# Two-layer hybrid decoder trunk on one core: low parts of the MLP's middle tiles on VectorE, and other buffers for the second pair of raw quad weights

## The chip, the cores and the metric

The kernel runs on one core of one Trainium2 chip. The metric is the device time of that core in microseconds (us), from a run of the whole program; lower is better. A core has a matrix engine (TensorE, PE in the profile), three engines for elementwise work (VectorE: DVE, ScalarE: ACT, GpSimd: POOL), and SyncE (SP), which here issues loads. Each engine has a queue of its own and works it off in order; between engines the program waits on semaphores. Matrix products accumulate in PSUM; all else lies in SBUF.

## The reference

Two layers (`DEPTH = 2`), a sequence of 512 tokens, model width 1024, everything in float32. Each layer mixes tokens with three parallel groups of heads and then runs an MLP; only the MLP is touched here:

```python
        x = x + mixed @ w_out[l]

        h = rms_norm(x, norm_mlp_g[l])
        x = x + jnp.square(jax.nn.relu(h @ w_mlp_up[l])) @ w_mlp_down[l]
    return rms_norm(x, final_norm_g)
```

`w_mlp_up` is 1024 x 4096, `w_mlp_down` 4096 x 1024.

## The kernel before

**Layout and precision.** Activations lie transposed: a tile is 128 features by 512 tokens, so x is 8 tiles, the middle of the MLP 32 tiles ("mids"). A float32 product is made of three matmuls on a shorter format: each operand is split into a high part (a cast, on ScalarE) and a low part (the operand less its high part, a subtraction of two SBUF tiles), and high x high, high x low and low x high are added up in PSUM. So every weight tile that is loaded costs a load on SyncE's queue, a cast on ScalarE and a subtraction, mostly on VectorE (`weights`, L333; `both`, L1488; `split` inside `quad`, L1577).

**Up projection.** The first four mids are plain products (`up`). The other 28 are made two at a time by `two` (L1478): a 2x2 scheme that needs seven half-size products where the plain one needs eight. It forms sums of weight blocks (s1 to s4; s1 and s3 of the later pairs come ready-made from an accumulating load that GpSimd issues, L1476), seven products into the PSUM tiles pa, pb and pc (12 matmuls of 256 columns each), and copies such as `c1`, which ScalarE takes out of PSUM (L1545) before the next product may accumulate further on pa. Then `square` applies relu, the norm's factor (VectorE, L1417) and the square (ScalarE, L1418), and `kept` (L1403) splits the mid into high part `mh` (ScalarE, L1408) and low part `ml` (L1409): for the first four mids of a layer on VectorE, for the other 28 on GpSimd.

**Down projection.** It runs in halves: `down(h, ...)` multiplies four mids (h counts 0 to 7) into four of the eight x tiles. For the (h, half) listed in `DN_QUADS`, six in layer 0 and four in layer 1, `quad` (L1573) does it with the same seven-product scheme; `turn_blocks` forms the sums of mids that it needs. Elsewhere plain products (dn) of 512 columns are used. A quad works on two pairs of x tiles, i = 0 and i = 1. For each pair it loads two raw weight tiles r0 and r1 (`rawq`, L1610), splits r0 (whi/wlo "a"), forms the sums s2q and s4q on VectorE (L1614 to L1618), splits those (shi/slo "b" and "c") and a part of r1 (whi/wlo "d"). The last reader of a pair's raw tiles is one of the sums or the low part "d". Then the products of both pairs run interleaved; p1q, p5q, u2q and c1q are copies from PSUM on ScalarE (L1599), and all additions to x are on VectorE.

**Buffers.** The four raw tiles of a quad come from the ring "raw" of three buffers of 128 x 512 float32, which the plain weights' raw tiles use too. A ring "sq" of two buffers of the same size holds squares of x for the norms: in the mixer, and at the end of the MLP (last down half of layer 0, last group of layer 1).

**Order.** The mixer's order of work is written out by hand (`ORDER`, with `SLOTS` for its buffers). The MLP's is not: the framework orders each engine's instructions when the program is built, from the order in the source and its own plan, so casts and sums of one product can stand ahead of copies of another, and parts of `two` and `quad` interleave.

Of the kernel before, what the change touches and what calls it, by code (L numbers as in the profile page):

```python
# [10 lines left out]
F32 = mybir.dt.float32  # L11
# [5 lines left out]
ALU = mybir.AluOpType  # L17
# [6 lines left out]
P = 128  # L24
# [249 lines left out]
def tile_trunk(ctx: ExitStack, tc: tile.TileContext, xT, wts, prm_d, cst_d, lora_d, gup_d, lam_d, fin_d, hd_d, out):  # L274
    nc = tc.nc
    act, dve, pool = nc.scalar, nc.vector, nc.gpsimd
# [23 lines left out]
    wp = Pool(ctx.enter_context(tc.tile_pool(name="wp", bufs=2)), "wp")  # L300
# [3 lines left out]
    def psum(tag, bufs, name):  # L304
        return ps.tile([P, 512], F32, tag=tag, bufs=bufs, name=name)
# [23 lines left out]
    WB = 3  # L329
# [238 lines left out]
    for l in range(L):  # L568
# [826 lines left out]
        with ExitStack() as mx:  # L1395
# [7 lines left out]
            def kept(m):  # L1403

                i = len(mids)
                hi = fp.tile([P, S], F32R, tag="mh", bufs=RING, name=f"mh{l}_{i}")
                lo = fp.tile([P, S], F32R, tag="ml", bufs=RING, name=f"ml{l}_{i}")
                act.copy(hi, m)  # L1408
                (dve if i < 4 else pool).tensor_tensor(lo, m, hi.bitcast(F32), ALU.subtract)  # L1409
                mids.append((hi, lo))  # L1410

            def square(cs, name, side=ALU.max):

                m = fp.tile([P, S], F32, tag="m", bufs=4, name=f"m{name}")
                for i, c in enumerate(cs):
                    q = slice(i * H, i * H + c.shape[1])
                    dve.scalar_tensor_tensor(m[:, q], c, 0.0, rs[:, q], side, ALU.mult)  # L1417
                act.activation(m, m, AF.Square)  # L1418
                kept(m)
                return m  # L1420
# [152 lines left out]
            def quad(h, half):  # L1573
# [3 lines left out]
                def split(src, pool_, tags, bufs, name):  # L1577
                    hi, lo = [pool_.tile([P, 4, P], F32R, tag=t, bufs=bufs, name=f"{t}{l}_{h}_{name}")[:, :src.shape[1]] for t in tags]
                    act.copy(hi, src)
                    dve.tensor_tensor(lo, src, hi.bitcast(F32), ALU.subtract)  # L1580
                    return hi, lo
# [23 lines left out]
                for i in range(2):  # L1605
                    j = 4 * half + 2 * i
                    n = f"{l}_{h}_{j}"
                    r0, r1 = [wp.tile([P, 4, P], F32, tag="raw", bufs=WB, name=f"rawq{n}_{c}") for c in range(2)]
                    for c, r in enumerate((r0, r1)):
                        nc.sync.dma_start(r.rearrange("p k c -> p (k c)"),  # L1610
                                          wts[wbase + NG_IN + NG_OUT + NG_UP + 8 * g + j + c, :, k0 * P:(k0 + 4) * P])
                    w0 = split(r0, wp, ("whi", "wlo"), WB, f"{j}a")
                    s = [fp.tile([P, 4, P], F32, tag=t, name=f"{t}q{n}") for t in ("s2", "s4")]
                    dve.tensor_tensor(s[0][:, :2], r1[:, 0::2], r1[:, 1::2], ALU.add)  # L1614
                    dve.tensor_tensor(s[0][:, 2:], s[0][:, :2], r0[:, 0::2], ALU.subtract)
                    s12 = split(s[0], fp, ("shi", "slo"), 5, f"{j}b")
                    dve.tensor_tensor(s[1][:, :2], r0[:, 0::2], r1[:, 0::2], ALU.subtract)
                    dve.tensor_tensor(s[1][:, 2:], r0[:, 1::2], s[0][:, 2:], ALU.subtract)  # L1618
                    s34 = split(s[1], fp, ("shi", "slo"), 5, f"{j}c")
                    w22 = split(r1[:, 1::2], wp, ("whi", "wlo"), WB, f"{j}d")  # L1620
                    pts = [psum(t, b, f"q{c}{n}")[:, :H] for c, t, b in zip("abc", (("rp", "rp", "at"), ("mm", "mm", "at"))[i],
                                                                          ((4, 4, 2), (2, 2, 2))[i])]
                    ab.append((j, w0, s12, s34, w22, pts))
                for step in ((0, 1), (2, 3), (5, 4), (6,)):
                    for j, w0, s12, s34, w22, (pa, pb, pc) in ab:
                        n = f"{l}_{h}_{j}"
# [28 lines left out]
            def down(h, js):  # L1655

                if (h, js[0] // 4) in DN_QUADS[l]:
                    quad(h, js[0] // 4)
                    return
                g, k0 = h // 2, 4 * (h % 2)  # L1660
                if h == 0 and js[0] == 0:
                    pts = [psum(("at", "mm")[j], 2, f"dn{l}_{h}_{j}") for j in js[:2]]
                    ws = [list(weights(wbase + NG_IN + NG_OUT + NG_UP + 8 * g + j, k0, k0 + 4)) for j in js[:2]]
                    for a, b in ((0, 3), (3, 4)):
                        for j, pt, w in zip(js, pts, ws):
                            for k in range(a, b):
                                (whi, wlo), (ahi, alo) = w[k], mids[k]
                                pe.matmul(pt, whi, ahi, start=(k == 0), stop=False)
                                pe.matmul(pt, whi, alo, start=False, stop=False)
                                pe.matmul(pt, wlo, ahi, start=False, stop=(k == 3))  # L1670
                    for j, pt in zip(js, pts):
                        dve.tensor_tensor(x[j], pt, x[j], ALU.add)
                    js = js[2:]
                for j in js:
                    pt = psum(*(("mm", 2), ("rp", 4))[j % 2], f"dn{l}_{h}_{j}")
                    mm3(pt, weights(wbase + NG_IN + NG_OUT + NG_UP + 8 * g + j, k0, k0 + 4), mids[4 * h:4 * h + 4], 4)
                    dve.tensor_tensor(x[j], pt, x[j], ALU.add)
                    if h == 2 * N_KG - 1 and j < NK - LATE:
                        norm_tile(j, f"m{l + 1}")
# [92 lines left out]
```

## Time and profile before

| | us |
|---|---|
| median of 3 runs | 1237.47 (1237.47 to 1239.9) |
| the profiled execution | 1238.0, its span 1236.2 |
| MLP of layer 0 in the span, about | 276 to 600 |
| MLP of layer 1, about | 900 to 1227 |

The rows that carry the argument stand in the prediction. In rows of groups, the number after the bar is the busy time, then the mean of one instruction in ns, then the idle time of its engine just before and what ended it. In rows of the timeline the first number is the start in us from the span's start, the second the duration; brackets hold the engine's idle time before it and what released it. In rows of windows: the length, then busy times of PE, PE's weight loads, DVE, ACT and POOL (with counts), the clock granted to TensorE as a share, the DMA engines' mean busy share and GB/s. In rows of waits: who <- for whom: us in total, times, longest.

### The profile page before, as it was taken

The page shows a single profiled execution, that of the slowest core. Times are in us where ns is not written, and L with a number is a line of the kernel's source. Part 1 is how long each engine was busy: PE and PEld are TensorE (multiplying, and loading weights), DVE is VectorE, ACT ScalarE, POOL GpSimd, SP SyncE. Part 2 cuts the span into 40 slices and gives each one's busy share as a digit, 9 for nine tenths or more (in the row PEclk, how much of TensorE's full clock was granted, in tenths as well). Part 3 has the DMA queues.
Part 4 walks back from the last instruction along what each step waited for, and adds up shares of the span by engine and source line. Part 5 has one row for each costly group of instructions (what it writes and reads, how often), then busy time and mean ns, then how long its engine had stood idle before and what let it go on. Part 6 is the DMA issues. An engine that isn't in the chain of part 4 may idle for free. (4 is left out here: it accounts for less than half of the span.)

```text
span 1236.2 us, 26900 instructions
## 1 busy us (share of the span) xinstructions
PE 1217.8 (99%) x10090; PEld 1065.6 (86%) x10090; DVE 1011.3 (82%) x2023; ACT 742.6 (60%) x1606; POOL 386.0 (31%) x502
## 2 busy tenths in 40 slices
PE   9999999999999999999999999999999999999997
PEld 7788788888999989889888888888889898998987
DVE  7787888879888998989867777787897999899654
ACT  7785755557456655656675656564775566565543
POOL 2264636331122121121126354553302212222111
PEclk9999999999999999999999999999999999999998
DMA  6523333125653463631235243322456645446122
GB/s 225 159 90 108 111 86 102 53 96 169 190 146 108 128 180 98 168 86 52 94 113 159 82 133 118 94 70 69 145 172 147 152 110 158 128 118 177 54 78 77
DMA packets 95506, 148.48 MB, mean 120 GB/s; under 512 B 22544, under 2 KB 26384, under 8 KB 95376
## 3 DMA queue, kind: packets, MB, share of 16 engines
q1 hardware_dynamic: 87168, 132.39, 34.5%
q0 software_dynamic: 7488, 13.63, 7.2%
q8 instruction: 79, 1.29, 0.5%
q10 hardware_dynamic: 720, 0.75, 0.2%
q14 instruction: 51, 0.42, 0.1%
HBM read 137.56 MB, written 9.18 MB: 119 GB/s over the span
## 5 line engine op out<-in xcount | busy, mean ns | idle before, releaser
L694 POOL TENSOR_TENSOR wlo<-raw,whi 128x512 fp32r<-128x512 f32 x84 | 112.1, 1336 | 203.8 <-ACT whi L682 167.3
L287 PE MATMUL pj<-ahim,whi 128*128 128x512 f32 x392 | 156.7, 400 | 0.0
L287 PE MATMUL pj<-ahim,wlo 128*128 128x512 f32 x392 | 156.5, 399 | 0.0
L287 PE MATMUL pj<-alom,whi 128*128 128x512 f32 x392 | 156.0, 398 | 0.0
L1476 POOL DMA_DIRECT2D s<-wts x52 | 48.0, 922 | 293.3 <-DVE slo_p L1491 68.5
L1409 POOL TENSOR_TENSOR ml<-m,mh 128x512 fp32r<-128x512 f32 x56 | 82.3, 1518 | 178.9 <-ACT mh L1408 63.1
L682 ACT CAST whi<-raw 128x512 fp32r<-128x512 f32 x142 | 87.6, 618 | 70.3 <-PE pj L287 26.5
L287 PE MATMUL dn<-mh,whi 128*128 128x512 f32 x288 | 112.3, 390 | 0.0
L287 PE MATMUL dn<-ml,whi 128*128 128x512 f32 x288 | 112.2, 390 | 0.0
L287 PE MATMUL dn<-mh,wlo 128*128 128x512 f32 x288 | 112.1, 390 | 0.0
L1490 ACT CAST shi_p<-s 128x512 fp32r<-128x512 f32 x112 | 70.0, 625 | 65.1 <-PE pa L287 35.1
L287 PE MATMUL pa<-thi,shi_p 128*128 128x256 f32 x336 | 95.6, 285 | 4.5 <-ACT c L1545 3.9
L287 PE MATMUL pa<-tlo,shi_p 128*128 128x256 f32 x336 | 94.8, 282 | 0.0
L287 PE MATMUL pa<-thi,slo_p 128*128 128x256 f32 x336 | 94.4, 281 | 0.0
L1491 DVE TENSOR_TENSOR slo_p<-s,shi_p 128x512 fp32r<-128x512 f32 x112 | 76.5, 694 | 17.8 <-ACT shi_p L1490 16.6
L348 ACT CAST whi<-raw 128x512 fp32r<-128x512 f32 x86 | 52.9, 620 | 56.2 <-PE dn L287 30.7
L287 PEld LDWEIGHTS pj<-alom,whi 128*128 128x128 f32 x392 | 73.9, 188 | 14.0 <-issue 0.5
L287 PEld LDWEIGHTS pj<-ahim,wlo 128*128 128x128 f32 x392 | 73.9, 188 | 13.8 <-issue 0.2
L287 PEld LDWEIGHTS pj<-ahim,whi 128*128 128x128 f32 x392 | 73.8, 188 | 13.7 <-issue 0.3
L349 DVE TENSOR_TENSOR wlo<-raw,whi 128x512 fp32r<-128x512 f32 x86 | 72.5, 846 | 10.7 <-ACT whi L348 10.7
L1490 ACT CAST shi_p<-raw 128x512 fp32r<-128x512 f32 x84 | 52.4, 624 | 33.6 <-PE pb L287 18.1
L287 PEld LDWEIGHTS pa<-thi,shi_p 128*128 128x128 f32 x336 | 63.0, 188 | 6.1 <-ACT c L1545 4.7
(649 smaller groups left out, 3905.2 us busy)
## 6 DMA issues: line engine op xcount, KB each, us to landing
raw<-wts SPq DMA_DIRECT2D x323, 256.0 KB, 2.8
s<-wts SPq DMA_DIRECT2D x52, 256.0 KB, 3.6
s<-wts POOLq DMA_DIRECT2D x52, 256.0 KB, 4.4
rawq<-wts SPq DMA_DIRECT2D x40, 256.0 KB, 2.9
qs<-dqhi SPq DMA_DIRECT2D x24, 128.0 KB, 3.4
ks<-dkhi SPq DMA_DIRECT2D x24, 128.0 KB, 3.6
x<-xT SPq DMA_DIRECT2D x8, 256.0 KB, 4.8
dqhi<-qhi SPq DMA_DIRECT2D x6, 256.0 KB, 3.2
```

Source lines behind the costliest of these rows:

```text
L287: ins = nc.tensor.matmul(*a, **k)
L348: act.copy(hi[:, :n], raw[:, :n])
L349: (pool if a and lean[0] else dve).tensor_tensor(lo[:, :n], raw[:, :n], hi[:, :n].bitcast(F32), ALU.subtract)
L682: yield act.copy(hi[:, k0:k1], raw[:, k0:k1])
L694: yield eng.tensor_tensor(lo[:, k0:k1], raw[:, k0:k1], hi[:, k0:k1].bitcast(F32), ALU.subtract)
L1409: (dve if i < 4 else pool).tensor_tensor(lo, m, hi.bitcast(F32), ALU.subtract)
L1476: pool.dma_start(t.rearrange("p k c -> p (k c)"), of[1], accum_op=ALU.add)
L1490: act.copy(hi, src)
L1491: dve.tensor_tensor(lo, src, hi.bitcast(F32), ALU.subtract)
```

## The change

Two lines. In `kept`, the low part of every mid is made on VectorE, so 28 subtractions a layer change their engine. In `quad`, the raw tiles r0 and r1 of the second pair (i = 1) come from the ring "sq" with its two buffers; those of the first pair stay in "raw" with its three.

```diff
                 act.copy(hi, m)
-                (dve if i < 4 else pool).tensor_tensor(lo, m, hi.bitcast(F32), ALU.subtract)
+                dve.tensor_tensor(lo, m, hi.bitcast(F32), ALU.subtract)
                 mids.append((hi, lo))
...
                 for i in range(2):
                     j = 4 * half + 2 * i
                     n = f"{l}_{h}_{j}"
-                    r0, r1 = [wp.tile([P, 4, P], F32, tag="raw", bufs=WB, name=f"rawq{n}_{c}") for c in range(2)]
+                    r0, r1 = [wp.tile([P, 4, P], F32, tag=("raw", "sq")[i], bufs=(WB, 2)[i], name=f"rawq{n}_{c}") for c in range(2)]
```

No other line changes; the number of matmuls, loads, casts and subtractions is the same.

## The prediction

> **What bounds the kernel now.** I read the head of the page first, then TensorE's own waits, then the windows by stage, then the groups on VectorE and GpSimd, and at the end the order of time around two of the waits.
>
> ```profile
> span 1236.2 us, 26900 instructions
> PE 1217.8 (99%) x10090; PEld 1065.6 (86%) x10090; DVE 1011.3 (82%) x2023; ACT 742.6 (60%) x1606; POOL 386.0 (31%) x502
> ```
>
> TensorE is busy for all but 18.4 us of the span, and the change removes no matmul. So it can only win back stalls of TensorE, or add some. Where those 18.4 us lie (columns: PE, PEld, DVE, ACT, POOL busy):
>
> ```profile
> 276.00:600.00 324.00, 319.75 (x2212) 297.02 (x2211) 290.97 (x535) 195.00 (x396) 66.40 (x57) 1.00 0.48 131
> 900.00:1181.00 281.00, 277.34 (x1931) 258.67 (x1930) 241.92 (x437) 162.71 (x332) 58.94 (x51) 1.00 0.50 133
> 1227.00:1236.20 9.20, 1.70 (x16) 1.32 (x16) 2.84 (x12) 1.52 (x4) 1.62 (x3) 0.67 0.59 194
> ```
>
> The two MLP stretches, the only ones that the diff touches, lose 4.25 and 3.66 us; 7.5 us are the output tail, which stays. VectorE is 90% busy in the first stretch. Who is late is in the list of TensorE's waits:
>
> ```profile
> PE pa L287 <- ACT c L1545: 3.9, 4, 1.2
> PE qa L287 <- ACT p1q L1599: 2.9, 4, 0.9
> ```
>
> So there are eight stalls that matter, 6.8 us together, all behind a PSUM copy on ScalarE. They come as pairs: p1q inside a second quad of an h, c some 15 us later. One place in order of time shows what such a stall costs in full:
>
> ```profile
> 434.04 0.28 PE L287 MATMUL pb<-alof,shi_p 128*128 128x256 f32 x1
> 434.15 0.28 PE L287 MATMUL pb<-ahif,slo_p 128*128 128x256 f32 x1
> 435.34 0.39 PE L287 MATMUL pa<-thi,shi_p 128*128 128x256 f32 x1 [0.91 <-ACT c L1545]
> 435.56 0.28 PE L287 MATMUL pa<-tlo,shi_p 128*128 128x256 f32 x1
> ```
>
> Such matmuls run at a step of about 0.12 (434.04 to 434.15). Here the steps are 1.19 and then 0.22: 1.07 + 0.10 = 1.17 lost, where the list says 0.91. With 0.26 more for each, the eight cost 6.8 + 8 x 0.26 = **8.9 us**: about all that can be won.
>
> **Why ScalarE is late: two causes.** First p1q:
>
> ```profile
> 410.05 0.33 SPq L343 DMA_DIRECT2D raw<-wts  x1
> 410.42 0.43 SPq L1610 DMA_DIRECT2D rawq<-wts  x1
> ```
> ```profile
> 414.88 0.43 DVE L1614 TENSOR_TENSOR s2q<-rawq 128x256 f32<-128x256 f32 x1 [2.05 <-DMA rawq<-wts]
> ```
> ```profile
> 416.06 0.62 ACT L1579 CAST shi_6b<-s2q 128x512 fp32r<-128x512 f32 x1 [3.83 <-DVE s2q L1615]
> 417.40 0.62 ACT L1408 CAST mh<-m 128x512 fp32r<-128x512 f32 x1
> 418.75 0.62 ACT L1408 CAST mh<-m 128x512 fp32r<-128x512 f32 x1
> 419.79 0.37 ACT L1599 COPY p1q<-qa 128x256 f32<-128x256 f32 x1
> ```
>
> The last raw tile of the quad's second pair is asked for at 410.42 only, because three "raw" buffers hold four tiles and this one waits for the sums of the first pair (L1618) to let go. VectorE stands 2.05 us for it, ScalarE 3.83 behind that. ScalarE then works off a row without a gap, and p1q, whose matmuls were over, is copied at 419.79; TensorE waits for it.
>
> Then c:
>
> ```profile
> 433.59 0.69 DVE L1499 TENSOR_TENSOR s<-s,raw 128x512 f32<-128x512 f32 x1
> ```
> ```profile
> 434.39 0.62 ACT L1490 CAST shi_p<-s 128x512 fp32r<-128x512 f32 x1 [2.22 <-PE pb L287]
> 434.92 0.37 ACT L1545 COPY c<-pa 128x256 f32<-128x256 f32 x1
> ```
>
> ```profile
> 414.88:434.28 19.40, 18.72 (x155) 18.26 (x153) 19.40 (x38) 13.41 (x30) 4.09 (x3) 1.00 0.43 124
> ```
>
> The view names PE as the releaser of that cast, but it reads a sum s that VectorE finished at 434.28, so I put it to VectorE. In the window from 414.88 to there VectorE is busy 19.40 of 19.40 us: it is a backlog. The copy of c stands behind that cast in ScalarE's queue.
>
> **Part 1: 56 low parts of mids go from GpSimd to VectorE.** What they cost today and what they disturb:
>
> ```profile
> L1409 POOL TENSOR_TENSOR ml<-m,mh 128x512 fp32r<-128x512 f32 x56 | 82.3, 1518 | 178.9 <-ACT mh L1408 63.1 <-DVE wlo_2d L1580 32.4 <-issue 28.4
> L1409 DVE TENSOR_TENSOR ml<-m,mh 128x512 fp32r<-128x512 f32 x8 | 5.5, 689 | 0.5 <-ACT mh L1408 0.5
> L349 DVE TENSOR_TENSOR wlo<-raw,whi 128x512 fp32r<-128x512 f32 x86 | 72.5, 846 | 10.7 <-ACT whi L348 10.7
> L1499 DVE TENSOR_TENSOR s<-s,raw 128x512 f32<-128x512 f32 x28 | 27.0, 965 | 0.0
> L1499 DVE TENSOR_TENSOR s<-raw,s 128x512 f32<-128x512 f32 x28 | 25.1, 895 | 0.4
> L1566 DVE TENSOR_TENSOR dlo<-ta,dhi 128x512 fp32r<-128x512 f32 x10 | 9.8, 984 | 0.0
> L1561 DVE TENSOR_TENSOR ta<-m,ta 128x256 f32<-128x256 f32 x10 | 9.6, 959 | 0.0
> L1562 DVE TENSOR_TENSOR tb<-m,m 128x256 f32<-128x256 f32 x10 | 9.2, 921 | 0.0
> L1580 DVE TENSOR_TENSOR wlo_6d<-rawq,whi_6d 128x256 fp32r<-128x256 f32 x5 | 7.5, 1509 | 0.0
> ```
> ```profile
> 323.86 3.85 DVE L349 TENSOR_TENSOR wlo<-raw,whi 128x512 fp32r<-128x512 f32 x1
> 396.59 0.42 DVE L1580 TENSOR_TENSOR wlo_2d<-rawq,whi_2d 128x256 fp32r<-128x256 f32 x1
> 410.27 0.68 DVE L1580 TENSOR_TENSOR wlo_6a<-rawq,whi_6a 128x512 fp32r<-128x512 f32 x1
> 410.88 0.42 DVE L1541 TENSOR_TENSOR c<-pc,p 128x256 f32<-128x256 f32 x1
> 416.82 0.42 DVE L1417 SCALAR_TENSOR_TENSOR m<-c,rsf 128x256 f32<-128x256 f32 x1
> 418.76 1.46 DVE L1499 TENSOR_TENSOR s<-s,raw 128x512 f32<-128x512 f32 x1
> 420.14 1.51 DVE L1580 TENSOR_TENSOR wlo_6d<-rawq,whi_6d 128x256 fp32r<-128x256 f32 x1
> ```
> ```profile
> 418.16 3.21 POOL L1409 TENSOR_TENSOR ml<-m,mh 128x512 fp32r<-128x512 f32 x2 [5.32 <-PE qc L287]
> ```
>
> *Added*: back to back, a 128x512 subtraction advances VectorE by 0.60 (410.27 to 410.88; its record of 0.68 overlaps the next). 56 x 0.60 = 33.6 us; by the record's 0.689 it would be 38.6. I take 0.60, since the queue is what counts.
> *Given back*: VectorE's instructions with two SBUF inputs stretch while GpSimd computes. The two at 418.76 and 420.14 lie on GpSimd's pair (418.16 to 421.37) and take 1.46 for 0.69 and 1.51 for 0.43; the one at 323.86 took 3.85. Over the groups, (mean less 0.689, or 0.43 for 256 columns) x count: L349 13.5, L1499 7.7 and 5.8, L1566 3.0, L1561 5.3, L1562 4.9, wlo_6d 5.4: **45.6 us**. All of it can't be charged with certainty to these 56, so the bounds are 0 and 45.6; I take 45.6, since each group is an MLP line and GpSimd has no other arithmetic there. VectorE's net is 33.6 - 45.6 = **12 us less** in the two stretches, by the other end 33.6 more.
>
> The Trainium skill, page "SBUF — State Buffer", section on engine ports, says that VectorE and GpSimd lock a shared port pair for a whole instruction, and that an instruction of VectorE with two SBUF inputs blocks against one of GpSimd that reads SBUF. The 3.85 us at 323.86 agree. By that rule alone each of the 56 could block VectorE for up to 1.518, 85 us; the rows show about half, since many start beside instructions that read PSUM. Against this, the skill's "VectorE: DVE Perf Modes" gives (N+151)/0.96 ns for such an instruction, 691 ns at 512: an estimate of 56 x 0.691 = 38.7 us added and 7 us net saved. The record agrees with that length, but the queue advances by 0.60.
>
> *Moved*: the 56 leave GpSimd's queue, where they stood ahead of the accumulating loads of s; those can only start earlier. A new ml on VectorE waits for its copy mh on ScalarE. Behind it stand c0q, the sums s and slo_p, on which casts and TensorE wait. If ml stands right behind the m that is squared, it waits: VectorE was through m at 417.24 (416.82 + 0.42), the copies end at 418.02 and 419.37, so some 0.8 + 0.75 = 1.5 us a pair, and nothing if it stands later. The matmuls that read ml come a half of the down projection later, so its delay itself costs nothing. I take 0.3 a pair on the path in the quads' stretches, nearer to none, because the eight that VectorE does already idled 0.5 us in all (row above).
>
> **Part 2: raw tiles of the second pair in "sq".** No instruction is added. Those two buffers were last read by wlo_2d of the quad before, at 396.59 (row above), so the load of 410.42 can go up to 13 us earlier. VectorE's waits of this kind:
>
> ```profile
> DVE s2q L1614 <- DMA rawq<-wts: 9.5, 6, 2.4
> ```
>
> I expect 8 to 9.5 of these to go (nothing if SyncE reaches the load no earlier). "sq" is otherwise used in the MLP only for norms at its end, when no quad runs. In layer 0, twelve tiles change ring; twelve is a multiple of 2 and 3, so the later buffers stay the same.
>
> **The sum.** The p1q stalls, 2.9 + 4 x 0.26 = 3.9, go with the late tile. The c stalls, 3.9 + 4 x 0.26 = 4.9, go if VectorE is over 1.1 us earlier at 433.59: 2.05 of gap and (0.77 + 1.08 - 1.2) = 0.65 of contention make 2.7, less 0.3 for new waits. That is 8.9. Against it I set 2 us for new stalls: a rebuilt order on three engines, 28 pairs, a quarter of them with 0.3 us. What is late next is the tail, and TensorE itself. 1238.0 (the profiled execution) - 6.9 = **1231** us; the median of the three runs, 1237.47, is 0.5 lower, within what the estimate can tell.
>
> **The rivals.**
> *Only the tile part works* (the backlog stays because ml waits about as long as the contention it removes): 1238.0 - 3.9 = 1234. For it: VectorE is 90% busy. Against it: 2.7 us of slack where 1.1 is needed.
> *The change doesn't do what it says*: SyncE's queue is in order, and the load of the last raw tile stays behind others that wait (the one before it, 410.05, waits too), or gains and new stalls cancel: 1236 to 1239, say 1238.
> *Slower: head of line on VectorE.* With every pair of ml right behind m, 1.5 us of wait plus 1.2 of work against 1.85 of contention is 0.85 a quad; in ten quads, where VectorE has no gap, 8.5 us; less 3.9 of part 2: 1242.6. It decides from about 0.65 us of wait a pair on. For it: m, square, copy and ml are a chain, and a planned order can put ml early. Against it: VectorE has 9.5 us of waits to fill.
>
> **How the numbers follow.** Forecast, 1228.5 to 1233.5: 0.50. Tile part only, 1233.5 to 1235.5: 0.17. No change, 1235.5 to 1239.5: 0.17. Slower, about 1242.6: 0.16. A measurement of this kernel can tell about 0.2%, 2.5 us. Below 1235.0 lie the forecast and three quarters of the second case: faster 0.63; slower 0.15; same 0.22. The range runs from 1228, all eight stalls gone and the small ones too, to 1241, which leaves out about 0.13 above and little below; the likeliest case's own is 1228.5 to 1233.5.
>
> **What would show it.** Part 1 right: no VectorE record over 1 us in the MLP, mean of L349 near 0.69, GpSimd's busy time 82 lower, VectorE's 0 to 15 lower. Part 2 right: the wait of s2q for rawq gone. The sum right: both rows, c and p1q, gone from TensorE's waits and PE idle in the two stretches below 3 us. Wrong: a new row "ml <- ACT mh" of 10 us and more on VectorE, with TensorE behind it.

## The result and the profile after

| | median, us | runs | ratio to before (95% interval) |
|---|---|---|---|
| before | 1238.68 (1237.47 to 1241.7) | 4 | |
| changed | 1230.22 (1227.54 to 1230.97) | 4 | 0.9924 (0.9898 to 0.995) |
| changed, measured again on the chip of the first experiments (before there: 1237.72) | 1229.59 | 5 | 0.9936 (0.9923 to 0.9948) |

The kernel became faster by 0.8% in the first measurement and by 0.6% in the second (8.5 and 8.1 us): little, but both intervals lie clear of 1. The profiled execution took 1229.54 us, 8.46 less than the one of before (1238.0). The head of the page after:

```profile
span 1227.7 us, 26836 instructions
PE 1216.4 (99%) x10090; PEld 1065.5 (87%) x10090; DVE 999.1 (81%) x2079; ACT 743.9 (61%) x1606; POOL 306.8 (25%) x446
```

TensorE's busy time is nearly the same (1217.8 before): of the 8.5 us, 7.1 are idle time of TensorE (18.4 before, 11.3 now). VectorE has 56 instructions more (2079 for 2023) and is busy 12.2 us *less*; GpSimd is busy 79 us less. TensorE's waits after, in the stretch of the two MLPs and the mixer between (from 276 to 1181 us):

```profile
PE up L287 <- DVE wlo L349: 0.4, 1, 0.4
PE dn L287 <- DVE ml L1409: 0.3, 1, 0.3
PE dn L287 <- ACT mh L1408: 0.2, 1, 0.2
```

The rows of c (3.9 us, 4 times) and p1q (2.9, 4) are gone, and so are two that the prediction does not count, p (0.6) and c1q (0.2). The three rows left are new, 0.9 us together, at the head of layer 1's MLP (897 to 908 us). The same two stretches as before, by windows (length, then PE, PEld, DVE, ACT, POOL busy); the changed kernel is some us ahead, so they hold a little more of its work:

```profile
276.00:600.00 324.00, 324.00 (x2237) 301.52 (x2237) 286.83 (x571) 199.99 (x402) 27.13 (x29) 1.00 0.50 133
900.00:1181.00 281.00, 280.51 (x1948) 261.85 (x1947) 237.97 (x461) 163.19 (x330) 21.72 (x25) 1.00 0.50 130
```

TensorE idled 4.25 and 3.66 us there, now 0.00 and 0.49: 7.4 of the 8.5 us. Next, VectorE's groups after, in the order line, names, shape, count, busy, mean of one in ns:

```profile
L349 DVE TENSOR_TENSOR wlo<-raw,whi 128x512 fp32r<-128x512 f32 x86 | 58.2, 683 | 4.9 <-ACT whi L348 4.9
L1409 DVE TENSOR_TENSOR ml<-m,mh 128x512 fp32r<-128x512 f32 x64 | 43.5, 685 | 2.5 <-ACT mh L1408 2.1
L1499 DVE TENSOR_TENSOR s<-s,raw 128x512 f32<-128x512 f32 x28 | 20.1, 718 | 0.0
L1499 DVE TENSOR_TENSOR s<-raw,s 128x512 f32<-128x512 f32 x28 | 19.2, 686 | 0.3
L1566 DVE TENSOR_TENSOR dlo<-ta,dhi 128x512 fp32r<-128x512 f32 x10 | 6.8, 681 | 0.0
L1562 DVE TENSOR_TENSOR tb<-m,m 128x256 f32<-128x256 f32 x10 | 4.2, 418 | 0.0
L1561 DVE TENSOR_TENSOR ta<-m,ta 128x256 f32<-128x256 f32 x10 | 4.2, 417 | 0.0
```

The groups that were stretched are back at their undisturbed length: L349 went from a mean of 846 to 683 ns, L1561 from 959 to 417. (The 718 holds one record of 1.67 us at the head of layer 0's MLP; the median is 684.) The 64 ml waited 2.1 us in all for mh. And the place where c was late, in order of time after, on ScalarE, then on VectorE and TensorE:

```profile
430.72 0.62 ACT L1490 CAST shi_p<-s 128x512 fp32r<-128x512 f32 x1 [0.53 <-ACT u L1534]
432.23 0.37 ACT L1545 COPY c<-pa 128x256 f32<-128x256 f32 x1 [0.89 <-PE pa L287]
432.75 0.62 ACT L1490 CAST shi_p<-s 128x512 fp32r<-128x512 f32 x1 [0.15 <-DVE s L1499]
```
```profile
431.98 0.68 DVE L1499 TENSOR_TENSOR s<-s,raw 128x512 f32<-128x512 f32 x1
```
```profile
433.45 0.28 PE L287 MATMUL pa<-thi,shi_p 128*128 128x256 f32 x1
```

The copy of c now waits for TensorE, as it should, and no longer stands behind the cast of s. Two things have changed. First, the sum s is ready sooner against TensorE's work: it ends at 432.66, 0.79 us before TensorE goes on with pa at 433.45; before, it ended at 434.28, just when pa was due (434.15 + 0.12). Second, the rebuilt program has a new order: the copy is now in front of the cast. With the cast in front, as before, the copy would end at about 432.75 + 0.53 + 0.37 = 433.65, some 0.2 us too late; that is an estimate from these rows, with 0.53 from the start of a cast to that of the copy behind it (434.39 to 434.92 before). So by this estimate the earlier sum covers most of this stall, and the order the rest. The other three places of c look the same.

### The profile page after: what moved, and what is told of

It is laid out like the page before. It is cut to its first block, busy times and chain, and to the rows that moved or that the text cites. A ratio compares the mean times of both kernels' runs of the same rounds, so it can differ in the third digit from the quotient of the medians.

```text
span 1227.7 us, 26836 instructions
## 1 busy us (share of the span) xinstructions
PE 1216.4 (99%) x10090; PEld 1065.5 (87%) x10090; DVE 999.1 (81%) x2079; ACT 743.9 (61%) x1606; POOL 306.8 (25%) x446
## 4 chain that ended last, share of the span: by engine, by line
PE 92%; DVE 2%; ACT 2%; DMA 1%; issue 1%; SPq 0%; POOL 0%; POOLq 0%; ACTq 0%; DVEq 0%
PE pj L287 21%; PE dn L287 16%; PE pa L287 13%; PE po L287 8%; PE pb L287 7%; PE qa L287 5%; PE dnF L287 4%; PE pc L287 3%; PE qb L287 2%; PE up L287 2%; PE sc L287 1%; PE ptt L292 1%; PE qc L287 1%; PE pg L287 1%; PE pyy L287 1%
## 5 line engine op out<-in xcount | busy, mean ns | idle before, releaser
L694 POOL TENSOR_TENSOR wlo<-raw,whi 128x512 fp32r<-128x512 f32 x84 | 112.8, 1344 | 262.3 <-ACT whi L682 230.6
L348 ACT CAST whi<-raw 128x512 fp32r<-128x512 f32 x86 | 53.2, 620 | 60.2 <-PE dn L287 45.6
L1677 DVE TENSOR_TENSOR x<-dn,x 128x512 f32<-128x512 f32 x68 | 46.7, 687 | 29.2 <-PE dn L287 29.2
L1491 DVE TENSOR_TENSOR slo_p<-raw,shi_p 128x512 fp32r<-128x512 f32 x84 | 57.6, 687 | 8.2 <-ACT shi_p L1490 7.3
L287 PEld LDWEIGHTS dn<-mh,whi 128*128 128x128 f32 x288 | 54.1, 188 | 11.7 <-ACT mh L1408 0.7
```

The source lines that it names most:

```text
L287: ins = nc.tensor.matmul(*a, **k)
L348: act.copy(hi[:, :n], raw[:, :n])
L694: yield eng.tensor_tensor(lo[:, k0:k1], raw[:, k0:k1], hi[:, k0:k1].bitcast(F32), ALU.subtract)
```

## The experiments

Two questions: which half of the change took which stall, and whether GpSimd's arithmetic is what stretched VectorE. My theory had two causes that add: the late raw tile makes p1q late, and VectorE's backlog makes c late. The rivals: contention alone is the cause; the place of ml in the order is; VectorE pays for the added work. One more rival has no run of its own, but the traces bear on it: each edit makes the framework order the engines' queues anew, and a stall can go with that order alone.

| run | median, us | ratio to before (95% interval) |
|---|---|---|
| changed, again | 1229.59 | 0.9936 (0.9923 to 0.9948) |
| part 1 alone | 1232.19 | 0.9954 (0.9941 to 0.9968) |
| part 2 alone | 1232.62 | 0.9959 (0.9945 to 0.9973) |
| with GpSimd's twin subtraction | 1239.37 | 1.0013 (1.0004 to 1.0022) |
| with GpSimd's zeros | 1230.52 | 0.9937 (0.9922 to 0.9952) |
| without ml | 1229.72 | 0.9932 (0.9917 to 0.9947) |
| three tiles open | 1230.12 | 0.9938 (0.9924 to 0.9951) |

The first four were compared with a before of 1237.72 us, the last three with one of 1238.15.

**The changed kernel again.** No edit.

> The changed kernel as it is, on the chip of the runs beside it, so that the two halves of the change can be compared with it. Every theory expects 0.990 to 0.995 of the kernel before, as measured already (0.9924).

It is the yardstick: 1229.59 us.

**Part 1 alone: ml on VectorE.**

```diff
-                (dve if i < 4 else pool).tensor_tensor(lo, m, hi.bitcast(F32), ALU.subtract)
+                dve.tensor_tensor(lo, m, hi.bitcast(F32), ALU.subtract)
```

> Part 1 alone: all low parts ml on VectorE, all four raw quad tiles in the ring raw as before. My theory (two causes that add): the raw tile of the second pair is still late, so the p1q stalls stay (3.9 us for four with their aftershocks); VectorE keeps its 2 us gap for that tile and wins only about 0.65 us a quad from the contention, less than the 1.1 that the c stalls need, so these shrink from 1.2 to about 0.5 us each. Gain 2 to 4 us: 1234.5 to 1236.5 where before has 1238. Rival 1 (contention with GpSimd is the whole cause, the tiles do nothing): both kinds of stalls go, gain 8 to 9 us, 1229 to 1230. Rival 2 (moving ml costs VectorE more than it wins): no gain or slower, 1238 and up, with a row of VectorE's waits ml <- ACT mh of 10 us or more.

It gained 5.5 us (1237.72 - 1232.19), between my figure (2 to 4) and that of rival 1 (8 to 9). TensorE's waits of this run, 276 to 1181, and then two rows of VectorE's:

```profile
PE qa L287 <- ACT p1q L1599: 0.9, 1, 0.9
PE dn L287 <- DVE ml L1409: 0.5, 2, 0.3
```
```profile
DVE s2q L1614 <- DMA rawq<-wts: 7.4, 5, 2.9
DVE ml L1409 <- ACT mh L1408: 3.1, 9, 0.6
```

All c stalls are gone, and three of the four p1q stalls too, though VectorE still waits 7.4 us for the late tile. So the lateness alone did not stall TensorE. First p1q, in the same quad as in the prediction, on VectorE, on ScalarE, and on TensorE:

```profile
414.66 0.42 DVE L1614 TENSOR_TENSOR s2q<-rawq 128x256 f32<-128x256 f32 x1 [1.16 <-DMA rawq<-wts]
```
```profile
415.84 0.62 ACT L1579 CAST shi_6b<-s2q 128x512 fp32r<-128x512 f32 x1 [2.80 <-DVE s2q L1615]
419.57 0.37 ACT L1599 COPY p1q<-qa 128x256 f32<-128x256 f32 x1
```
```profile
420.33 0.28 PE L287 MATMUL qa<-dhi,shi_6b 128*128 128x256 f32 x1
```

The gap is 1.16 us here, 2.05 before; p1q is copied by 419.94 and TensorE wants it at 420.33, with 0.4 us to spare. Before, the copy ended at 420.16 and TensorE stood 0.53. The sums that let the raw buffer go are themselves VectorE's work, and two of the instructions ahead of them took 1.63 and 1.45 beside GpSimd's ml at 397. Against TensorE's first matmul on qa with shi_4b (418.09 before, 418.89 here), the load of the tile is asked for 0.47 us sooner (410.42 before, 410.75 here) and s2q starts 1.02 us sooner. So contention had made part of the tile's lateness; why the load itself was quicker as well is not shown. The order of ScalarE's queue in front of p1q is the one of before, so here the order is not what helped.

With c it is. ScalarE at the place of c:

```profile
433.15 0.37 ACT L1545 COPY c<-pa 128x256 f32<-128x256 f32 x1 [0.89 <-PE pa L287]
434.79 0.62 ACT L1490 CAST shi_p<-s 128x512 fp32r<-128x512 f32 x1 [1.26 <-DVE s L1499]
```

TensorE goes on with pa at 434.37. The sum s ends only at 434.70, later against TensorE than before the change, and a copy behind that cast could not have started before 435.3. All four places look like this one: with part 1 alone the c stalls went because the copy moved in front of the cast, not because VectorE caught up. Rival 2 is out: 3.1 us of waits for mh, and faster.

**Part 2 alone: second pair in "sq".**

```diff
-                    r0, r1 = [wp.tile([P, 4, P], F32, tag="raw", bufs=WB, name=f"rawq{n}_{c}") for c in range(2)]
+                    r0, r1 = [wp.tile([P, 4, P], F32, tag=("raw", "sq")[i], bufs=(WB, 2)[i], name=f"rawq{n}_{c}") for c in range(2)]
```

> Part 2 alone: second pair of raw quad tiles in sq, the 56 low parts ml still on GpSimd. My theory: the wait of s2q for rawq goes, the four p1q stalls go (3.9 us); the 2 us that VectorE no longer stands exceed the 1.1 that the c stalls need, so these go too or nearly: gain 6 to 9 us, 1229 to 1232, and part 1 is then worth 0 to 2 us on top. VectorE's long records (over 1 us) beside ml on GpSimd stay. Rival 1 (contention is the cause): p1q stalls stay or move, gain under 2 us, 1236 and up. Rival 2 (the two causes are separate): p1q goes and c stays, gain about 4 us, 1234.

It gained 5.1 us, less than the 6 to 9 of my theory and more than the 4 of rival 2. TensorE's waits, 276 to 1181, the longest two, and some of VectorE's groups:

```profile
PE qa L287 <- ACT p1q L1599: 1.4, 4, 0.4
PE pa L287 <- ACT p L1522: 0.7, 1, 0.7
```
```profile
L349 DVE TENSOR_TENSOR wlo<-raw,whi 128x512 fp32r<-128x512 f32 x86 | 69.4, 810 | 9.4 <-ACT whi L348 9.3
L1499 DVE TENSOR_TENSOR s<-raw,s 128x512 f32<-128x512 f32 x28 | 28.4, 1016 | 0.4
L1561 DVE TENSOR_TENSOR ta<-m,ta 128x256 f32<-128x256 f32 x10 | 12.5, 1250 | 0.8 <-ACT m L1418 0.8
```

VectorE's wait for rawq is gone, as expected, and so are all c stalls, with contention still there (1250 ns for L1561, where 417 is undisturbed). But p1q did not go: it halved, and moved to the first pair of the quad (shi_4b). TensorE there, and ScalarE's queue ahead of it:

```profile
421.12 0.38 PE L287 MATMUL qa<-dhi,shi_4b 128*128 128x256 f32 x1 [0.35 <-ACT p1q L1599]
```
```profile
418.31 1.15 ACT L1418 ACTIVATE m<-m 128x512 f32<-128x512 f32 x2
419.37 1.13 ACT L1408 CAST mh<-m 128x512 fp32r<-128x512 f32 x2
420.39 0.40 ACT L1579 CAST whi_6d<-rawq 128x256 fp32r<-128x256 f32 x1
420.70 0.63 ACT L1599 COPY p1q<-qa 128x256 f32<-128x256 f32 x2
```

With the tile in time, the order puts both squares and both casts of the mids ahead of p1q. ScalarE works this row off without a gap from 417.27 on, behind the cast of VectorE's s4q, which ended at 417.16. The changed kernel has the same row in the same order, but its s4q ends 0.4 us sooner against TensorE (4.01 us before the matmul on qa with shi_4b; here 3.61 before that matmul was due). So VectorE's backlog now reaches p1q by this way.

And ScalarE at the place of c:

```profile
435.09 0.62 ACT L1490 CAST shi_p<-s 128x512 fp32r<-128x512 f32 x1 [0.81 <-DVE s L1499]
435.62 0.36 ACT L1545 COPY c<-pa 128x256 f32<-128x256 f32 x1
```

Here the cast still stands in front, and the copy is over at 435.98, 0.40 us before TensorE goes on with pa at 436.38: the sum came in time. But it is another sum (s<-raw,s, where before it was s<-s,raw), since VectorE's order is new too, so this run does not tell whether VectorE's lead or the order did it.

The halves gain 5.5 + 5.1 = 10.6 us, the whole 8.1 (1237.72 - 1229.59). Each of these gains is uncertain by some 1.6 us (half its interval), so they alone hardly tell the difference. TensorE's idle time in the two stretches does, in the profiled executions: it falls from 7.91 us to 2.21 with part 1, to 3.43 with part 2 and to 0.49 with both. That is 5.7 + 4.5 = 10.2 for the halves against 7.4: they overlap, since each alone ends the c stalls.

**GpSimd's arithmetic put back.** The changed kernel, and GpSimd repeats the subtraction into a scratch tile.

```diff
                 dve.tensor_tensor(lo, m, hi.bitcast(F32), ALU.subtract)
+                if i >= 4:
+                    scratch = wp.tile([P, S], F32, tag="acc", bufs=1, name=f"scr{l}_{i}")
+                    pool.tensor_tensor(scratch, m, hi.bitcast(F32), ALU.subtract)
```

> The changed kernel, and beside each of the 56 ml on VectorE GpSimd makes the same subtraction once more, into a scratch tile that nothing reads. So GpSimd's arithmetic is back while VectorE has the work as well. My theory (GpSimd's arithmetic stretches VectorE's instructions with two SBUF inputs): records over 1 us are back in the MLP, 35 to 50 us in all over their undisturbed length, VectorE is overloaded in the quads' stretches and TensorE's stalls return: 1236 to 1250. Rival (the long records came from the place of ml in the order, not from GpSimd's arithmetic): no records over 1 us, 1229 to 1232.

1239.37 us: all of the gain is gone, 9.8 us over the changed kernel. TensorE's first wait, GpSimd's group and two of VectorE's, whose line numbers below the edit are three higher:

```profile
PE qa L287 <- ACT p1q L1602: 7.5, 5, 1.6
```
```profile
L1412 POOL TENSOR_TENSOR scr<-m,mh 128x512 f32<-128x512 f32 x56 | 99.7, 1780 | 174.7 <-ACT mh L1408 108.9 <-DVE c0q L1637 63.5
```
```profile
L349 DVE TENSOR_TENSOR wlo<-raw,whi 128x512 fp32r<-128x512 f32 x86 | 70.9, 832 | 3.9 <-ACT whi L348 3.9
L1409 DVE TENSOR_TENSOR ml<-m,mh 128x512 fp32r<-128x512 f32 x64 | 61.9, 973 | 2.0 <-ACT mh L1408 1.7
```

VectorE's busy time is 1043.1 us on that run's page, 43.7 over the changed kernel's 999.4 in the run beside it, for the same VectorE instructions; ml itself went from a mean of 690 to 973 ns. Nobody reads or waits for the scratch tile. So GpSimd's arithmetic does stretch VectorE. This stretch reaches TensorE by p1q: in the quad above, ScalarE's order in front of p1q is that of the changed kernel, and TensorE stands 1.57 us for p1q where it had not stood at all. The rival that the order alone made the long records falls. ScalarE at the place of c shows why c does not stall here:

```profile
435.14 0.37 ACT L1548 COPY c<-pa 128x256 f32<-128x256 f32 x1 [0.89 <-PE pa L287]
436.67 0.62 ACT L1493 CAST shi_p<-s 128x512 fp32r<-128x512 f32 x1 [1.16 <-DVE s L1502]
```

The sum s is late again, after TensorE has gone on with pa at 436.36, but the copy of c stands in front of its cast.

**GpSimd writes but does not read.** As above, with this line instead:

```diff
-                    pool.tensor_tensor(scratch, m, hi.bitcast(F32), ALU.subtract)
+                    pool.memset(scratch, 0.0)
```

> As the run with GpSimd's twin subtraction, but GpSimd only fills the scratch tile with zeros, 56 times, reading nothing from SBUF. Theory A (what stretches VectorE is GpSimd's reading, as the Trainium skill, SBUF - State Buffer, has it for instructions with two SBUF inputs): no VectorE record over 1 us in the MLP, the time of the changed kernel, 1228 to 1232. Theory B (any GpSimd instruction on SBUF does it): long records again, by the length of the fill, and 1232 to 1238.

1230.52 us, no change, and no stretch (L349 has a mean of 684 ns). The fills hardly wait for anything, so they run in rows at the head of each MLP; one stretch of it on GpSimd, and on VectorE beside it:

```profile
291.07 8.91 POOL L1412 MEMSET scr<- 128x512 f32 x15
```
```profile
293.06 0.68 DVE L1409 TENSOR_TENSOR ml<-m,mh 128x512 fp32r<-128x512 f32 x1
294.37 0.68 DVE L1409 TENSOR_TENSOR ml<-m,mh 128x512 fp32r<-128x512 f32 x1
297.98 0.68 DVE L349 TENSOR_TENSOR wlo<-raw,whi 128x512 fp32r<-128x512 f32 x1
```

Instructions with two SBUF inputs keep 0.68 us beside fills. That favours theory A. The Trainium skill, page "SBUF — State Buffer", section "Who interferes with whom", has it so: a VectorE instruction with two SBUF inputs contends with a GpSimd instruction that reads SBUF, not with one that only writes it. The time of this run says less, because the fills did not fall into the quads.

**ml left out.** What does VectorE's added work itself cost? This kernel leaves out the 56 low parts, and the products take the high part in their place, so the matmuls stay as many.

```diff
-                lo = fp.tile([P, S], F32R, tag="ml", bufs=RING, name=f"ml{l}_{i}")
+                lo = fp.tile([P, S], F32R, tag="ml", bufs=RING, name=f"ml{l}_{i}") if i < 4 else hi
...
-                dve.tensor_tensor(lo, m, hi.bitcast(F32), ALU.subtract)
+                if i < 4:
+                    dve.tensor_tensor(lo, m, hi.bitcast(F32), ALU.subtract)
```

> The changed kernel with the 56 low parts left out: the products of those mids take the high part twice, so matmuls and their number stay, and neither VectorE nor GpSimd makes ml. My theory (the 33.6 us that ml adds to VectorE lie beside TensorE's work and cost nothing): 1228 to 1230, as the changed kernel within 0.15%; VectorE's busy time falls by 34 to 39. Rival (VectorE's added work still costs): 1222 to 1227.

1229.72 us, ratio 0.9932 where the changed kernel has 0.9936 and 0.9924. Its page:

```profile
PE 1215.6 (99%) x10090; PEld 1065.5 (87%) x10090; DVE 965.8 (79%) x2023; ACT 744.6 (61%) x1606; POOL 306.9 (25%) x446
```

VectorE works 33.3 us less (999.1 - 965.8) than in the changed kernel, close to the 33.6 of the sum (just under the 34 to 39 expected), and the time does not tell. The added work is hidden.

**Three tiles open at the head of the down projection**, to cover the new waits for mh and ml.

```diff
-                    pts = [psum(("at", "mm")[j], 2, f"dn{l}_{h}_{j}") for j in js[:2]]
-                    ws = [list(weights(wbase + NG_IN + NG_OUT + NG_UP + 8 * g + j, k0, k0 + 4)) for j in js[:2]]
+                    pts = [psum(*(("at", 2), ("mm", 2), ("rp", 4))[j], f"dn{l}_{h}_{j}") for j in js[:3]]
+                    ws = [list(weights(wbase + NG_IN + NG_OUT + NG_UP + 8 * g + j, k0, k0 + 4)) for j in js[:3]]
...
-                    js = js[2:]
+                    js = js[3:]
```

> The changed kernel, and in the first half of the down projection of each layer three x tiles instead of two are begun before the fourth mid is needed. In the trace of the changed kernel TensorE stands some 0.4 + 0.5 us there in layer 1 (for mh and ml of the fourth mid), 0.3 to 0.6 in layer 0. Theory: nine more matmuls of 0.227 us cover it, gain 0.8 to 1.5 us, 1228 to 1229. Rival: the third tile's weights must be cast and split earlier, VectorE is late for those instead, no gain or 1 us slower.

1230.12 us, no change, where my theory had a gain of 0.8 to 1.5. Its only wait of TensorE from 276 to 1181:

```profile
PE dn L287 <- DVE wlo L349: 0.9, 1, 0.9
```

The rival had it: the waits for up, ml and mh (0.9 us together) became one of 0.9 us for the low part of weights.

## Why the prediction was right, step by step

- **The bound.** Right. Matmuls stayed, and 7.4 of the 8.5 us are TensorE's idle time in the two MLP stretches; the forecast had said that about 8.9 were to be had there. With ml left out altogether no stall over 0.2 us is left there, and the time is the same: the MLP stretches have hardly more to give. The profiled execution gained 8.46 where the sum had 6.9: fewer new stalls came (below), and p and c1q went too, which the sum leaves out.
- **VectorE's net.** Forecast 12 us less, measured 12.2 (1011.3 - 999.1). Both terms held: 33.3 us of work by the run without ml, and so 12.2 + 33.3 = 45.5 us given back, where the forecast took the upper end of its bounds, 45.6. The run with GpSimd's twin has 43.7 us of stretch; that is of another order of work, so it is a check of size only. A small slip: GpSimd does have other arithmetic in the first stretch, three instructions of 4.1 us at its start (L694, L765, L373), and they stay.
- **The new wait.** 0.3 us a pair was too much: the 64 ml waited 2.1 us in all. The slower rival, ml head of line, did not come up.
- **The tile.** Right that the wait of s2q for rawq (9.5 us) would go; it did, in the changed kernel and with part 2 alone.
- **Which stall hangs on what.** This step failed, without moving the sum: "The p1q stalls ... go with the late tile. The c stalls ... go if VectorE is over 1.1 us earlier". Part 2 alone only halved p1q (2.9 to 1.4); part 1 alone, with the tile still late, took three of its four stalls. And the c stalls went with either half. The p1q stalls hang on VectorE's backlog, which the late tile and the contention each feed; the two don't add, and one feeds the other, since stretched sums let the raw buffer go later.
- **How much earlier VectorE gets to c.** This term of the same step was too large: 2.7 less 0.3, so 2.4 us, were forecast, and 1.1 needed. Against TensorE's work, the sum came 0.8 us earlier in the changed kernel, and in part 1 alone it came later than before. The c stalls went all the same: in part 1 alone by the rebuilt order, which put the copy of c in front of the cast, and in the changed kernel, by the estimate above, in part by it. The prediction reckons with a new order only as a source of new stalls; that it helped with the old ones was luck.
- **The rival "only the tile part works".** Its size (1234) is near what part 2 alone has (1232.62), but its picture, p1q gone and c left, was the wrong way round.
- **New stalls.** 2 us were set aside; the rows show 0.9 at the head of layer 1's MLP, or 1.7 with the prediction's 0.26 for each of three. In the changed kernel's second trace such waits come to 1.9 us.

Why those three came up is open: that the order there changed is only argued. What the smaller load on VectorE alone would have done to c is open too: no run has the smaller load and all queues in the order of before.

## What to carry to other kernels

Before moving work off a busy engine, look at what the other engine's instructions do to its records: a mean well above the least length of the same shape, at the times of the other's work, is load too, and it can exceed the work itself. Two causes that feed one queue don't add: test each alone, and don't expect the halves to sum to the whole. Where an edit makes the program's order anew, compare the order of the queues, run by run, before you put a stall's end down to the cause you had in mind. When a ring holds fewer buffers than one step loads, look for its lateness in what releases the buffer, not in the load.

## What the runs showed of the hardware that was not expected

VectorE and GpSimd disturb each other both ways: beside VectorE's own ml, GpSimd's twin subtraction of 128x512 took 1780 ns on average, with records from 1615 to 2813 ns, where ml had 1518 on GpSimd in the kernel before. (The scratch tile is plain float32, so the two are not quite alike.) GpSimd's fills (543 ns for 128x512 in their group's mean) left VectorE's records beside them at their length.

```profile
L1412 POOL MEMSET scr<- 128x512 f32 x56 | 30.4, 543 | 8.8 <-PE pssf L287 6.0
```
